# Decoder layer: output product in blocks of 512 columns scaled on VectorE, later routing pieces, first expert weights loaded from the last row tile, a unit of four experts last with its down weights in halves

## The chip, the cores and the metric

One core of one Trainium2 chip. The metric is the device time of one launch in microseconds, median of several runs. TensorE multiplies, VectorE and ScalarE work elementwise, GpSimd too, SyncE (SP) issues most of the transfers; each engine takes its instructions in the order in which the program wrote them. The profile's granted clock of TensorE is given as a share of its full speed.

## What is computed

One layer for a single sequence of 512 tokens of width 1024, float32. Two token mixers (a gated linear recurrence, HGRN2, and a sparse attention, NSA) are merged by sigmoid gates and go through one output product; then comes a mixture of experts, 32 experts in 4 groups, each token in 2 experts of its best group. The tail of the reference, which is what the change touches:

```python
merged = jax.nn.sigmoid(mg_h) * (o_h @ w_br_hg[l]) + jax.nn.sigmoid(mg_n) * (o_n @ w_br_nsa[l])
y = (1 + g1[:, None]) * (merged @ w_out[l])
x = _layer_norm(ALPHA * x + y) * ln1_g[l] + ln1_b[l]
h = _layer_norm(x) * (1 + sc2[:, None]) + sh2[:, None]
y = (1 + g2[:, None]) * _hier_moe(h, ...)      # softmax over groups, top 1; top 2 experts in it; SwiGLU
x = _layer_norm(ALPHA * x + y) * ln2_g[l] + ln2_b[l]
```

## The kernel before

Products of float32 precision are made of three TensorE passes: each operand is split into a rounded part and the rest (`wh`, `wl` for weights; ScalarE copies the rounded part, L275, VectorE subtracts it, L276), and `three_k` issues high by high, high by low and low by high. A `Block` holds the weights of one block of columns; it is loaded in pieces of 512 KB (`wst`), `np` pieces of `kp` row groups each. Weights with `early=True`, those of the output product `wo`, are first multiplied by the row 1 + g1 (`g1b`) on GpSimd, L274.

`run_jobs` runs a list of jobs in order and makes ready, beside each, the next blocks: their loads and splits are written between the matmuls of the jobs ahead. The last jobs are four merges of the first branch (`br_job(MGH, ...)`), the split of the attention's output (`onl`, L963), four merges of the second branch (`br_job(MGN, ...)`, which leave the merged rows split as `mh` and `ml`, L1091 and L1092) and the output product of row tile 0. `wo` is four blocks of 256 columns with two pieces each; two of these pieces are made ready in each of the four `MGN` merges.

Then a loop over the four row tiles of 128 tokens: `out_piece` makes the product of a tile with each of the four blocks of 256 columns (24 matmuls each), adds it to the residual `z` and takes statistics, for every 512 columns in the tiles 0 to 2, for every 256 in the last. After each tile but the last, its `ln` is spawned: LayerNorm 1, statistics of the second norm, eight transposes of `z` (`pzT`), logits (`plg`), choice of group and experts, rank of each token in its expert. `ln` is a generator; after each `yield` it goes on only when the planner's clock `W.clk`, which counts the estimated matmul time in ns, is later by the number yielded: `LN_T` (1000) ahead of the transposes, `LN_P` (3500) ahead of the logits, `LN_Q` and `LN_R` behind. `W.poll()` is called between pieces of the product. The last tile's `ln` (`last`) runs alone once all is drained.

Expert weights lie in the same 36 buffers of 128x1024 float32 (`Q`) as all else; a load is issued by SP, in order, and waits there until its buffer is free. The first unit's first four steps (eight loads) stand ahead of the loop over row tiles, the next (`load_unit((0, 1), LOADS[-1], 8, ...)`, eight loads) behind it, the first of these waiting for a buffer that the row tile 2 frees (`acc` out of `z`, L1203). The last four steps of the unit come after the last tile's routing.

Thirteen units follow, `[-2, -1] + ORDER`. The units -2 and -1 take the experts 0 to 3 in pairs, with 64 slots each; the others take the remaining experts by their number of tokens: 0 and 1 one expert with 128 slots, 2 to 6 two experts, 7 to 10 four experts with 32 slots each. All 32 experts are read, 12 loads of 512 KB each (`w1`, `w3`, `w2`, four steps each). `up` makes the SwiGLU product, `down` the second product, `combine` adds it to the rows (`acc`); for every second unit the rows of the next two units are gathered (`one_hots`, `gather`). The last unit is 6, two experts; its `w2` comes in quarters of 256 columns, rows of 1 KB, and the product, its scaling by weight and gate (`weighted_halves`) and the addition go quarter by quarter. Ahead of the last quarter's additions stands a loop for tokens beyond a unit's slots, which here runs no time (`overflow`). LayerNorm 2 closes the rows in eight pieces of 128x512, spread over VectorE, ScalarE and GpSimd by the list `CLOSE`; its gain and bias are read as two rows spread over 128 partitions by the DMA (`l2g`, `l2b`).

## Time and profile before

| | |
|---|---|
| time, median of 3 runs | 1269.35 us (1267.79 to 1269.76) |
| the profiled execution | 1270.81 us, span from the first to the last instruction 1268.6 us |
| TensorE busy | 1173.5 us (93%) |
| VectorE busy | 704.3 us (56%) |
| ScalarE busy | 427.2 us (34%) |
| GpSimd busy | 114.9 us (9%) |
| moved by DMA | 297.15 MB, of it expert weights 380 issues of 512 KB and some smaller |
| mean granted clock of TensorE | 0.982 |

A share over the whole span says little here, since the stages have different limits; the rows below are read by stretches of the span. Times in the rows are microseconds from the start of the span; where rows group instructions, the mean of one is in ns.

### The profile page before, as it was taken

What the parts mean: (1) busy time and instruction counts of PE and PEld (TensorE: products, weight loads), DVE (VectorE), ACT (ScalarE), POOL (GpSimd) and SP (SyncE); (2) the same over time, 40 slices, a digit from 0 to 9 for tenths busy, and PEclk for the clock granted to TensorE, in tenths of its full rate; (3) what the DMA queues carried; (4) which work ended last, traced back from release to release, by engine and by line L of the source; (5) the groups of instructions that cost most, each with busy time, mean ns of one, the idle gap of its engine ahead of it and who ended that gap; (6) DMA issues with size and microseconds to landing.
All of it is one profiled execution on the core that took longest, in us unless ns stands there. A gap on an engine that the chain in (4) does not pass through costs nothing. (4 is left out here: it accounts for less than half of the span.)

```text
span 1268.6 us, 18573 instructions
## 1 busy us (share of the span) xinstructions
PE 1173.5 (93%) x6647; PEld 813.2 (64%) x6647; DVE 704.3 (56%) x1645; ACT 427.2 (34%) x899; POOL 114.9 (9%) x176
## 2 busy tenths in 40 slices
...
GB/s 323 298 145 148 113 59 117 99 93 129 106 112 118 72 163 104 100 117 185 119 84 166 34 293 378 409 409 409 409 409 408 409 409 403 409 409 404 408 322 68
DMA packets 140926, 297.15 MB, mean 234 GB/s; under 512 B 11163, under 2 KB 83043, under 8 KB 140832
## 3 DMA queue, kind: packets, MB, share of 16 engines
...
q10 hardware_dynamic: 768, 2.37, 0.6%
...
q14 instruction: 41, 0.34, 0.1%
...
## 5 line engine op out<-in xcount | busy, mean ns | idle before, releaser
L183 PE MATMUL p<-ew,xe 128*32 128x512 f32 (+1 forms) x960 | 202.6, 597 | 14.0 <-DMA ew<-in_exp_w_dram 13.6
L276 DVE TENSOR_TENSOR wl<-wst,wh 128x1024 fp32r<-128x1024 f32 (+1 forms) x93 | 124.3, 1365 | 74.9 <-ACT wh L275 74.0
L183 PEld LDWEIGHTS p<-ew,xe 128*32 128x32 f32 (+1 forms) x960 | 54.1, 122 | 156.1 <-issue 80.4
L1514 DVE TENSOR_TENSOR s<-s,p 128x512 f32<-128x512 f32 x13 | 8.9, 688 | 189.3 <-PE p L183 173.6
L183 PE MATMUL py<-ew,aT 128*32 128x512 f32 (+2 forms) x496 | 98.8, 570 | 8.7 <-DMA ew<-in_exp_w_dram 5.9
L275 ACT ACTIVATE wh<-wst 128x1024 fp32r<-128x1024 f32 (+1 forms) x94 | 93.3, 1030 | 28.2 <-POOL wst L274 16.6
L183 PEld LDWEIGHTS py<-ew,aT 128*32 128x32 f32 (+1 forms) x496 | 27.1, 122 | 73.4 <-issue 33.4
L1522 ACT ACTIVATE aT<-pat 128x512 f32<-128x512 f32 x13 | 7.8, 597 | 186.5 <-PE pat L187 186.5
L1563 DVE TENSOR_TENSOR acc<-acc,pcb 128x512 f32<-128x512 f32 x96 | 58.3, 681 | 8.8 <-PE pcb L181 8.8
L1537 ACT ACTIVATE yh<-y 128x512 fp32r<-128x512 f32 (+1 forms) x28 | 16.8, 601 | 136.8 <-DVE y L1535 136.7
L181 PE MATMUL pgx<-pm,xhh 128*128 128x256 f32 (+1 forms) x224 | 55.7, 294 | 0.0
L181 PE MATMUL pgx<-pm,xhl 128*128 128x256 f32 (+1 forms) x224 | 54.2, 287 | 0.0
L514 POOL DMA_DIRECT2D adaw<-in_ada_w_dram x64 | 34.6, 543 | 195.6 <-PE ptp L187 43.7
L1535 DVE SCALAR_TENSOR_TENSOR y<-py,cs,g2b 128x512 f32<-128x512 f32 (+1 forms) x28 | 19.9, 711 | 58.4 <-PE py L183 58.2
L181 PE MATMUL pmg<-hh,wh 128*128 128x512 f32 x128 | 50.4, 394 | 0.0
L181 PE MATMUL psg<-hh,wh 128*128 128x512 f32 x128 | 50.3, 393 | 0.0
L181 PE MATMUL psg<-hl,wh 128*128 128x512 f32 x128 | 49.9, 390 | 0.0
L181 PE MATMUL pmg<-hh,wl 128*128 128x512 f32 x128 | 49.9, 390 | 0.0
L181 PE MATMUL psg<-hh,wl 128*128 128x512 f32 x128 | 49.9, 390 | 0.0
L181 PE MATMUL pmg<-hl,wh 128*128 128x512 f32 x128 | 49.8, 389 | 0.0
L181 PEld LDWEIGHTS pgx<-pm,xhh 128*128 128x128 f32 x224 | 43.6, 197 | 4.0 <-issue 2.3
L181 PE MATMUL pcb<-yh,pT 128*128 128x512 f32 (+1 forms) x112 | 43.7, 395 | 2.2 <-DVEq L1584 2.2
...
## 6 DMA issues: line engine op xcount, KB each, us to landing
ew<-in_exp_w_dram SPq DMA_DIRECT2D x380, 512.0 KB, 10.1
wst<-in_w_in_dram SPq DMA_DIRECT2D x66, 512.0 KB, 4.6
...
adaw<-in_ada_w_dram SPq DMA_DIRECT2D x16, 512.0 KB, 9.2
wst<-in_w_br_hg_dram SPq DMA_DIRECT2D x8, 512.0 KB, 6.6
wst<-in_w_br_nsa_dram SPq DMA_DIRECT2D x8, 512.0 KB, 4.4
wst<-in_w_out_dram SPq DMA_DIRECT2D x8, 512.0 KB, 4.5
...
```

The lines of the kernel that those rows point to most:

```text
L181: PE.matmul(o, l, r, start=start, stop=stop)
L183: PE.matmul(o, l, r, start=start, stop=stop, tile_position=pos)
L275: A.activation(wh, self.w[j], AF.Copy)
L276: (sub or V).tensor_sub(wl, self.w[j], wh.bitcast(F32))
L514: P_.dma_start(w, ada[:, k, 2048 + j * 512:2560 + j * 512])
L1514: V.tensor_mul(s1, s1, p3)
L1522: A.activation(aT, at_.rearrange("p (f s) -> p f s", f=4), AF.Copy)
L1535: V.scalar_tensor_tensor(y, py, cs_, g2b[c0 // 512][:, c0 % 512:c0 % 512 + n], op0=OP.mult, op1=OP.mult)
L1537: A.activation(yh, y, AF.Copy)
L1563: V.tensor_add(acc[i][:, s_], acc[i][:, s_], pc_)
```

## The change

The output product's weights become two blocks of 512 columns, with four pieces of two row groups each, and the multiplication by 1 + g1 moves from GpSimd to VectorE. The tiles 0 to 2 make two products of 512 columns, the last tile one of 512 and two of 256. `LN_T` goes from 1000 to 5000, `LN_P` from 3500 to 1500, and `proj_tok` with 512 columns yields after every second row group. The second batch of the first unit's loads is issued inside the last row tile, after its first 512 columns. In `ORDER` the unit 10, of four experts, comes last, and its `w2` is read in halves of 512 columns, two row groups to a load, rows of 2 KB. The last unit's rows are gathered inside the unit before it, between that unit's own two up products. Gain and bias of LayerNorm 2 are read as two rows of 4 KB, split, and spread over the partitions by TensorE. The end goes in two halves of 512 columns; the closing subtracts the mean and multiplies by the gain for whole rows on VectorE, then the tiles 0 and 1 are closed by a product with a diagonal matrix on TensorE, on top of the bias, and a copy by ScalarE, the tiles 2 and 3 by VectorE. `CLOSE` and GpSimd's part in it are gone. In the diff, a line of "..." marks what is left out.

```diff
@@ -65,15 +65,14 @@
...
-LN_T, LN_P, LN_Q, LN_L, LN_R = 1000, 3500, 800, 0, 3500
+LN_T, LN_P, LN_Q, LN_L, LN_R = 5000, 1500, 800, 0, 3500
...
-ORDER = [7, 0, 8, 1, 9, 2, 3, 10, 4, 5, 6]
+ORDER = [7, 0, 8, 1, 9, 2, 3, 4, 5, 6, 10]
...
-CLOSE = [(0, "VV"), (2, "AVP"), (3, "AVP"), (1, "VV"), (4, "AVP"), (6, "AVP"), (5, "VV"), (7, "VV")]
...
@@ -251,7 +250,7 @@
...
-            self.kp = {128: 8, 256: 4, 280: 2}[n]
+            self.kp = {128: 8, 256: 4, 280: 2, 512: 2}[n]
...
@@ -271,7 +270,7 @@
...
             if self.early:
-                P_.tensor_mul(self.w[j], self.w[j], g1b[:, None, self.c0:self.c0 + n].to_broadcast([128, kp, n]))
+                V.tensor_mul(self.w[j], self.w[j], g1b[:, None, self.c0:self.c0 + n].to_broadcast([128, kp, n]))
...
@@ -298,12 +297,12 @@
...
-    def proj_tok(b, ps, i, sh=None, sl=None, n=None):
+    def proj_tok(b, ps, i, sh=None, sl=None, n=None, c=0):
...
         for k in range(KT):
...
-                    lambda k: b.H(k, 0, n), lambda k: b.L(k, 0, n), k)
-            if k % 4 == 3:
+                    lambda k: b.H(k, c, n), lambda k: b.L(k, c, n), k)
+            if k % 4 == 3 or n == 512 and k % 2:
...
@@ -1100,7 +1099,7 @@
...
-    wo = [Block(vwo, c * 256, early=True) for c in range(4)]
+    wo = [Block(vwo, c * 512, 512, early=True) for c in range(2)]
...
@@ -1112,22 +1111,18 @@
...
-    def out_piece(b, i, q, width):
-        z, o = zs[i], q * 256 % width
-        if o == 0:
-            out_ps[i] = PS("pyo")[:, 0:width]
-        py = out_ps[i]
-        yield from proj_tok(b, py[:, o:o + 256], i, mh, ml)
-        if o + 256 == width:
-            s_ = slice(q * 256 + 256 - width, q * 256 + 256)
-            j = q * 256 // width
-            V.scalar_tensor_tensor(z[:, s_], z[:, s_], ALPHA, py, op0=OP.mult, op1=OP.add)
-            V.bn_stats(l1st[i][:, 6 * j:6 * j + 6], z[:, s_])
-    out_ps = {}
+    def out_piece(b, i, c, width):
+        z, n = zs[i], 256 if i + 1 == NT else 512
+        py = PS("pyo")[:, 0:width]
+        yield from proj_tok(b, py, i, mh, ml, width, c % 512)
+        s_ = slice(c, c + width)
+        V.scalar_tensor_tensor(z[:, s_], z[:, s_], ALPHA, py, op0=OP.mult, op1=OP.add)
+        for j in range(c // n, (c + width) // n):
+            V.bn_stats(l1st[i][:, 6 * j:6 * j + 6], z[:, j * n:(j + 1) * n])
...
-    jobs += [(wo[q], lambda b, q=q: out_piece(b, 0, q, 512), None) for q in range(4)]
+    jobs += [(wo[q], lambda b, q=q: out_piece(b, 0, q * 512, 512), None) for q in range(2)]
...
@@ -1287,7 +1282,7 @@
...
-    def load_unit(es, lo=0, hi=12, res=None, quarters=False):
+    def load_unit(es, lo=0, hi=12, res=None, halves=False):
...
         for t in range(lo, hi):
...
@@ -1302,10 +1297,11 @@
...
                 w = Q("ew")
-                if quarters and t >= 8:
-                    nc.sync.dma_start(w.rearrange("p (k n) -> p k n", k=4),
-                                      src.rearrange("p (k n) -> p k n", k=4)[:, :, j * 256:(j + 1) * 256])
+                if halves and t >= 8:
+                    kk, c0 = j % 2 * 2, j // 2 * 512
+                    nc.sync.dma_start(w.rearrange("p (k n) -> p k n", k=2),
+                                      src.rearrange("p (k n) -> p k n", k=4)[:, kk:kk + 2, c0:c0 + 512])
                 else:
                     nc.sync.dma_start(w, src[:, j * 1024:(j + 1) * 1024])
...
@@ -1319,14 +1315,16 @@
...
         if i:
-            for q in range(4):
-                for _ in out_piece(wo[q], i, q, width):
+            for c, w_ in ((0, 512), (512, 512)) if i + 1 < NT else ((0, 512), (512, 256), (768, 256)):
+                for _ in out_piece(wo[c // 512], i, c, w_):
...
+                if i + 1 == NT and c == 0:
+                    load_unit((0, 1), LOADS[-1], 8, w_first)
...
-    load_unit((0, 1), LOADS[-1], 8, w_first)
...
@@ -1601,7 +1599,7 @@
             combine(*down(act, {"exp_w2": [stream("exp_w2")]}, pw, lambda w, h: w(h)))
             for i in range(NT):
-                V.tensor_reduce(sums[:, i, 0:3], acc[i][:, 0:768].rearrange("p (q n) -> p q n", q=3), axis=AX.X, op=OP.add)
+                V.tensor_reduce(sums[:, i, 0:1], acc[i][:, 0:512], axis=AX.X, op=OP.add)
...
@@ -1623,8 +1621,26 @@
         def add_up():
             while todo:
                 combine(*todo.pop(0))
+        def next_hots():
+            nonlocal hots
+            for x in nxt:
+                rels[x] = rel_to(slots, 128.0 * x)
+            hots = one_hots([rels[x] for x in nxt])
         last = n + 1 == len(units)
-        act = up(xe, (n % 2) * 128, ws, mid=add_up if last else None)
+        nxt = units[n + 1:n + 3] if n % 2 == 1 else []
+        inside = len(nxt) == 1
+        xe_ = None
+        if inside:
+            next_hots()
+        def between():
+            nonlocal xe_
+            add_up()
+            if inside:
+                xe_ = gather(hots)
+        act = up(xe, (n % 2) * 128, ws, mid=between if last or inside else None)
         if last:
             break
         v_ = units[n + 1]
@@ -1636,119 +1652,122 @@
...
         else:
...
-        w_now, quarters = ws, n + 2 == len(units)
-        ws = load_unit(es, quarters=quarters)
+        w_now, halves = ws, n + 2 == len(units)
+        ws = load_unit(es, halves=halves)
...
-        nxt = units[n + 1:n + 3] if n % 2 == 1 else []
         def to_come():
-            nonlocal hots
...
-            if nxt:
-                for x in nxt:
-                    rels[x] = rel_to(slots, 128.0 * x)
-                hots = one_hots([rels[x] for x in nxt])
+            if nxt and not inside:
+                next_hots()
         todo.append(down(act, w_now, pw, mid=to_come))
         if nxt:
-            xe = gather(hots)
+            xe = xe_ if inside else gather(hots)
     w_now = ws
-    l2g = row_bc("l2g", a["ln2_g"])
-    l2b = row_bc("l2b", a["ln2_b"])
+    l2r = [Q(n_)[0:1, :] for n_ in ("l2gr", "l2br")]
+    for t, name in zip(l2r, ("ln2_g", "ln2_b")):
+        P_.dma_start(t, a[name])
...
-    sums = cp.tile([128, NT, 4], F32, name="sums")
+    sums = cp.tile([128, NT, 2], F32, name="sums")
...
-    def squares(i, half):
-        A.activation(sq, acc[i][:, half * 512:(half + 1) * 512], AF.Square, bias=nsh[:, i:i + 1],
-                     accum_out=sqs[:, i, half:half + 1])
-    def quarter_up(q):
-        py = PS("py")[:, 0:256]
+    halves_ = [slice(0, 512), slice(512, 1024)]
+    def squares(i, h):
+        A.activation(sq, acc[i][:, halves_[h]], AF.Square, bias=nsh[:, i:i + 1], accum_out=sqs[:, i, h:h + 1])
+    def half_up(h):
+        py = PS("py")
...
-                mm(py[m * x:m * x + m, :], aT[:, k, m * x:m * x + m], w[q][:, k * 256:(k + 1) * 256], k == 0, k == 3,
-                   pos=(0, m * x) if m < 128 else None)
+                mm(py[m * x:m * x + m, :], aT[:, k, m * x:m * x + m], w[2 * h + k // 2][:, k % 2 * 512:k % 2 * 512 + 512],
+                   k == 0, k == 3, pos=(0, m * x) if m < 128 else None)
...
-    def quarter_add(q, y, i):
-        pc_ = PS("pcb")[:, 0:256]
+    def half_add(h, y, i):
+        pc_ = PS("pcb")
...
-        z = acc[i][:, q * 256:(q + 1) * 256]
+        z = acc[i][:, halves_[h]]
...
-                               accum_out=sums[:, i, q:q + 1])
...
-    def quarter_y(q, py):
-        return weighted_halves(py, cs_, q * 256, 256)
-    py = quarter_up(0)
-    y = quarter_y(0, py)
...
+                               accum_out=sums[:, i, h:h + 1])
+    py = half_up(0)
+    y = weighted_halves(py, cs_, 0, 512)
+    oner = Q("oner", F32R)[0:1, 0:128]
+    A.activation(oner, ones[0:1, :], AF.Copy)
+    l2h, l2l = ([Q(n_, F32R)[0:1, :] for n_ in ns] for ns in (("l2gh", "l2bh"), ("l2gl", "l2bl")))
+    for t, h_, l_ in zip(l2r, l2h, l2l):
+        A.activation(h_, t, AF.Copy)
+        V.tensor_sub(l_, t, h_.bitcast(F32))
+    for i in range(NT):
+        half_add(0, y, i)
+    V.tensor_scalar(nsh, sums[:, :, 0], -1.0 / 512, None, op0=OP.mult)
+    l2g, l2b = Q("l2g"), Q("l2b")
+    for t, h_, l_ in zip((l2g, l2b), l2h, l2l):
+        for s_ in halves_:
+            ps = PS("pl2")
+            for j, x in enumerate((h_, l_)):
+                mm(ps, oner, x[:, s_], j == 0, j == 1)
+            A.activation(t[:, s_], ps, AF.Copy)
+    for i in range(NT):
+        squares(i, 0)
+    py = half_up(1)
+    y = weighted_halves(py, cs_, 512, 512)
     overflow()
...
-    V.tensor_reduce(l3[:, :, 4:5], sums[:, :, 0:3], axis=AX.X, op=OP.add)
     for i in range(NT):
-        quarter_add(3, y, i)
-    V.tensor_add(l3[:, :, 0], sums[:, :, 3], l3[:, :, 4])
+        half_add(1, y, i)
+        squares(i, 1)
+    V.tensor_add(l3[:, :, 0], sums[:, :, 0], sums[:, :, 1])
...
     V.tensor_mul(l3[:, :, 2], l3[:, :, 2], l3[:, :, 2])
     V.scalar_tensor_tensor(l3[:, :, 5], sqs[:, :, 0], 1.0 / D, l3[:, :, 2], op0=OP.mult, op1=OP.subtract)
...
-    for i in (0, 1):
-        squares(i, 1)
-    norm_scales(slice(0, 2))
-    for i in (2, 3):
-        squares(i, 1)
-    for j, (piece, how) in enumerate(CLOSE):
-        if j == 1:
-            norm_scales(slice(2, 4))
-        close(piece // 2, piece % 2, how)
+    def less_mean(i):
+        V.scalar_tensor_tensor(acc[i], acc[i], l3[:, i, 0:1], l2g, op0=OP.subtract, op1=OP.mult)
+    less_mean(0)
+    V.scalar_tensor_tensor(l3[:, :, 1], sqs[:, :, 1], 1.0 / D, l3[:, :, 5], op0=OP.mult, op1=OP.add)
+    A.activation(l3[:, :, 2], l3[:, :, 1], AF.Ln, bias=eps[:, 0:1])
+    A.activation(l3[:, :, 2], l3[:, :, 2], AF.Exp, scale=-0.5)
+    dg = S("dg")[:, 0:256].rearrange("p (i t) -> p i t", i=2)
+    pcl = {(i, h): PS("pcl") for i in range(2) for h in range(2)}
+    for (i, h), ps in pcl.items():
+        for j, b_ in enumerate((l2h[1], l2l[1])):
+            mm(ps, oner[:, 0:128], b_[:, halves_[h]], j == 0, False)
+    for i in range(2):
+        A.activation(dg[:, i, :], ident, AF.Copy, scale=l3[:, i, 2:3])
+    for i in range(1, NT):
+        less_mean(i)
+    for (i, h), ps in pcl.items():
+        z = acc[i][:, halves_[h]]
+        mm(ps, dg[:, i, :], z, False, True)
+        A.activation(z, ps, AF.Copy)
+        nc.sync.dma_start(out[0, i * 128:(i + 1) * 128, halves_[h]], z)
+    for i in range(2, NT):
+        for s_ in halves_:
+            z = acc[i][:, s_]
+            V.scalar_tensor_tensor(z, z, l3[:, i, 2:3], l2b[:, s_], op0=OP.mult, op1=OP.add)
+            nc.sync.dma_start(out[0, i * 128:(i + 1) * 128, s_], z)
...
```

## Rows read from the trace of the kernel before

**Rows 1.** Busy time by stretch: stretch, length, engines' busy us (instructions), clock, DMA share, GB/s.

```profile
582.00:625.00 43.00, 43.00 (x192) 35.37 (x190) 20.19 (x33) 15.66 (x16) 0.00 (x0) 1.00 0.34 110
625.00:681.35 56.35, 46.91 (x192) 36.90 (x192) 51.41 (x39) 15.41 (x18) 24.73 (x8) 0.94 0.39 127
681.35:745.70 64.35, 55.91 (x466) 53.85 (x464) 42.66 (x112) 20.08 (x32) 4.77 (x2) 0.97 0.37 130
744.00:746.00 2.00, 2.00 (x20) 1.88 (x18) 1.83 (x9) 1.97 (x3) 0.27 (x1) 1.00 1.04 422
745.70:764.60 18.90, 14.86 (x106) 13.58 (x104) 15.24 (x45) 8.18 (x13) 4.46 (x5) 0.73 1.02 373
776.00:1216.00 440.00, 414.98 (x2056) 179.03 (x2054) 171.09 (x404) 59.64 (x119) 0.28 (x1) 1.00 1.03 408
1216.00:1224.00 8.00, 8.00 (x37) 4.19 (x34) 2.73 (x5) 0.60 (x1) 0.78 (x2) 1.00 1.02 366
1224.00:1235.00 11.00, 9.83 (x54) 4.00 (x55) 3.45 (x6) 1.18 (x3) 0.00 (x0) 1.00 0.79 256
```

**Rows 2.** Groups of instructions, 625 to 681.35: count, busy us, mean ns, idle before.

```profile
L276 DVE TENSOR_TENSOR wl<-wst,wh 128x1024 fp32r<-128x1024 f32 x14 | 31.6, 2313 | 0.5 <-ACT wh L275 0.3 <-DMA wst<-in_w_out_dram 0.3
L274 POOL TENSOR_TENSOR wst<-wst,g1b 128x1024 f32<-128x1024 f32 x8 | 24.7, 3115 | 64.2 <-DVE onl L963 50.2 <-issue 7.3 <-DMA wst<-in_w_out_dram 6.7
L275 ACT ACTIVATE wh<-wst 128x1024 fp32r<-128x1024 f32 x12 | 11.9, 1046 | 16.6 <-POOL wst L274 16.6
```

**Rows 3.** Timeline of VectorE: start, us, instruction, count, idle before.

```profile
584.13 2.36 DVE L276 TENSOR_TENSOR wl<-wst,wh 128x1024 fp32r<-128x1024 f32 x2 [8.52 <-ACT wh L275]
...
630.08 13.43 DVE L276 TENSOR_TENSOR wl<-wst,wh 128x1024 fp32r<-128x1024 f32 x4
...
645.53 0.69 DVE L1092 TENSOR_TENSOR ml<-sgm,mh 128x512 fp32r<-128x512 f32 x1 [0.70 <-ACT mh L1091]
```

**Rows 4.** Timeline of TensorE in the second merge, its longest wait.

```profile
668.94 0.79 PE L181 MATMUL pbr<-onh,wl 128*128 128x512 f32 x1 [4.27 <-DVE wl L276]
```

**Rows 5.** Timeline of TensorE in the output product, two matmuls in a row.

```profile
700.49 0.28 PE L181 MATMUL pyo<-wh,ml 128*128 128x256 f32 x1
700.61 0.28 PE L181 MATMUL pyo<-wh,mh 128*128 128x256 f32 x1
```

**Rows 6.** TensorE's waits, 681.35 to 745.7: us in all, times, longest.

```profile
PE pzT L187 <- issue: 5.0, 2, 2.5
PE plg L183 <- ACT zT L1218: 2.1, 2, 1.1
```

**Rows 7.** Groups of the whole span (page, part 5), ScalarE's copy of 512 columns.

```profile
L1537 ACT ACTIVATE yh<-y 128x512 fp32r<-128x512 f32 (+1 forms) x28 | 16.8, 601 | 136.8 <-DVE y L1535 136.7
```

**Rows 8.** Timeline of VectorE, row tile 2 and the last tile.

```profile
733.04 1.28 DVE L1203 SCALAR_TENSOR_TENSOR acc<-z,l1mv,l1g 128x1024 f32<-128x1024 f32 x1
...
750.10 0.26 DVE L231 BATCH_NORM_AGGREGATE l1mv<-l1st 128x2 f32<-128x24 f32 x1
```

**Rows 9.** Waits of SP's DMA queue: us in all, times, longest.

```profile
SPq L1310 <- DVE acc L1203: 44.1, 1, 44.1
```

**Rows 10.** Timeline of VectorE and TensorE at the end.

```profile
1205.48 0.75 DVE L1535 SCALAR_TENSOR_TENSOR y<-py,cs,g2b 128x512 f32<-128x512 f32 x1 [2.51 <-PE py L183]
...
1221.27 4.87 DVE L1563 TENSOR_TENSOR acc<-acc,pcb 128x512 f32<-128x512 f32 x8 [8.77 <-PE pcb L181]
...
1233.82 3.67 PE L183 MATMUL py<-ew,aT 128*64 128x256 f32 x32 [0.31 <-ACT aT L1522]
...
1235.82 0.49 DVE L1535 SCALAR_TENSOR_TENSOR y<-py,cs,g2b 128x256 f32<-128x256 f32 x1 [0.74 <-PE py L183]
...
1248.43 0.17 DVE L1734 TENSOR_REDUCE l<-sums 128x4 f32<-128x12 f32 x1 [2.07 <-PE pcb L181]
...
1264.63 0.75 DVE L1707 SCALAR_TENSOR_TENSOR acc<-acc,l,l2b 128x512 f32<-128x512 f32 x1
```

**Rows 11.** DMA issues (page, part 6): count, size, median us to landing.

```profile
wst<-in_w_out_dram SPq DMA_DIRECT2D x8, 512.0 KB, 4.5
```

30 lines of the change are left out of this document (removed).

## The prediction

> **What bounds the kernel now.** I read the stages first, as busy time by stretch [rows 1]. From 776 to 1216 us the DMA engines move 408 GB/s at a share of 1.03, while TensorE, though called busy 94%, loads weights for only 179 of 440 us: the expert weights set the pace, every one of them is read whatever the routing, and the change removes none. So the time is where the stream starts, plus its bytes, plus what is left to do once it has ended. Before it lies a TensorE stage: the last merge of the branches (625.0 to 681.35) and the output product (681.35 to 745.7), 46.9 of 56.4 and 55.9 of 64.4 us busy. The merge of the other branch, the same 192 matmuls, took 43.0 us. Then a serial piece, 745.7 to 764.6, routes the last row tile. All weights that room can be found for are issued by 764.6, and the stream goes on only as the first unit uses buffers up, from 764.6. Hence the stream's end moves with that point, and an earlier load alone is worth nothing. At the end the last weights are in by 1235.0, and 33.6 us follow.
>
> **A. Scaling of the output weights on VectorE: +6.5 us.** GpSimd leaves the merge stage: 8 multiplies of 3.1 us, and beside them VectorE's 14 subtractions of 2.31 us on the mean [rows 2], where one alone takes 1.18 [rows 3]. But VectorE is in order, and it now does multiply, wait for ScalarE's copy, subtract: 1.2 (I take the subtraction's time) + 1.05 + 1.2 = 3.45 us a piece, 27.6 for eight. Blocks of 512 have four pieces, so all eight stand in the first two merge blocks; before, two pieces stood in each of four. VectorE comes out of the four `onl` at 630.1 [rows 3]. To the fourth block's first `wl` lie: 2.35 (two `wl` of the second block), 27.6, four merges of 0.69 + 0.69 + 0.70 waiting + 0.69 = 2.77 us [rows 3], together 11.1, the third block's copy and two `wl` less what overlaps, 2.7, and the fourth's copy and `wl`, 1.6. That is 45.3: 675.4. TensorE now waits for the same `wl` [rows 4] until 668.9, and has about 12.4 us of work behind it to 681.35, a slower clock included; so the stage ends near 687.8. Bounds: below, the twin stage's 43.0 us, a gain of 13.4; above, all eight subtractions still at 2.31, 9 us more, +15.5. I take the order of the code, +6.5.
>
> The Trainium skill (GPSIMD Engine Reference, section 4.1, Engine selection) says to put elementwise work on VectorE, since GpSimd is about twice as slow on two inputs. The rows agree on the instruction (3.1 against 1.2 us) and by that rule alone A would be a gain; it is the first rival.
>
> **B. Output product in 512 columns, routing later: -11.1 us.** A matmul of 256 columns starts 0.12 us after another [rows 5]: 384 are 46.1 us. One of 512 takes 43.0/192 = 0.224 [rows 1]: 168 of them and the 48 of 256 that the last tile keeps are 43.4, 2.7 less. TensorE idles 64.35 - 55.91 = 8.4 us in this stage [rows 1], 5.0 and 2.1 of it ahead of transposes and logits of the routing [rows 6] that were queued before VectorE or ScalarE had their input. With 5000 for 1000 on the planner's clock the transposes of a tile come a whole 512-column piece later (24 x 0.224 = 5.4 us), more than the 2.5 us that either wait lasted; the logits come 12 matmuls (2.7 us) behind, more than two copies of 0.6 us [rows 7]. I take all 8.4. Bounds: -2.7 (the waits only move) to -13.
>
> **C. The last tile's routing: +2.2 us.** Now the last row statistics start 4.4 us after TensorE's end [rows 8]. With the later delays the logits of the third tile come three quarters through the last piece, and their VectorE chain (L1228 to L1258, about 20 small instructions; 3.7 us, an estimate at 0.17 to 0.2 each, as the small one in [rows 10]) is queued ahead of the last residual add; the ranking of the third tile (1.7 to 3.3 us, an estimate for its nine by the same row) comes after it, and both ahead of the last statistics: 6.6 us. Bounds 0 and +4.
>
> So the first unit starts 6.5 - 11.1 + 2.2 = 2.4 us earlier. The second batch of eight loads is now held 44 us by buffers [rows 9]. In the change it is issued in the last row tile, about 10 us ahead of TensorE's end, as now (733.04 + 1.28 [rows 8], against 745.7): nothing won, but it must move along, since 20 loads and 1 MB of small ones (28 us at 408) have to fit before the first unit starts, and 30 us are there (734.4 to 764.6). Cover gone: each missing us is one us.
>
> **D. The stream itself: -7.5 us.** After 776 it carries 440 x 408 + 8 x 366 + 11 x 256 = 185.3 MB [rows 1]. Two broadcast rows of 0.5 MB each become two of 4 KB: 184.2 MB, at 408 GB/s 451.5 us, where it took 459.0. The slow end goes (256 GB/s at a share of 0.79 with rows of 1 KB): the last unit of four needs 61 us for its weights (48 of 512 KB) and some 29 of TensorE (144 matmuls at 415/2056 us), so loads no longer wait for TensorE, and its halves have rows of 2 KB, which moved 422 GB/s in the eight half-loads [rows 1]. Bounds: 0.4 more (no cost of the smaller rows) and 6 less (halves at 256/0.79 = 324 GB/s).
>
> **E. After the last weight: -12.3 us.** Now 33.6 us. In the change the first half's product, its adds and squares run while the last eight loads (10.3 us) arrive: 1.4 + 2.15 + 2.4 (two row splits) + 2.45 = 8.4 us on VectorE's side, hidden; if that cover is gone it costs what exceeds 10.3. After the landing: receipt 1.0 (an estimate, between 0 and the 3.2 us that hold a whole output after the last closing step, 1265.4 to the span's end [rows 10]), last matmuls 1.4 (between 0.5 and the 2.0 us that a whole quarter took from 1233.82 to 1235.82), y: 0.75 [rows 10] + 0.70 + 0.69 [rows 3] = 2.15, empty loop 2.1 (VectorE's idle time ahead of 1248.43), four adds at 4.87/8 = 0.61 [rows 10], five small ones 0.9, four subtractions of 1.28 [rows 8] at a step of 1.25 and one small 5.2, four closing halves at 0.7 (0.75 less what overlaps) 2.8, output 3.2: 21.2. ScalarE's squares end beside the small ones, and tiles 0 and 1 close on TensorE and ScalarE beside VectorE's subtractions (diagonal product and copy, four of each, ready some 1 us earlier than VectorE's last). GpSimd takes no part in it any more. The new matmuls that spread gain and bias (8) and their copies (4 of 0.6 us) lie ahead of the squares, in the same window. Bounds 18 and 27.
>
> **Sum.** 6.5 - 11.1 + 2.2 - 7.5 - 12.3 = -22.2 us on a span of 1268.6; the profiled run took 1270.81, 2.2 more, and the median of the runs lies 1.5 below it, at 1269.35. 1269.35 - 22.2 = 1247.
>
> **Rivals.**
> (1) The scaling is hidden: VectorE's chain keeps ahead of TensorE and A is a gain of about 11, 1230 us. For: GpSimd's contention goes, and ScalarE waited 16 us on it. Against: the order of the chain above. 12%.
> (2) The row tiles stay at their pace, since VectorE, not the order, sets it: 42.7 us busy in the product's 64.4 says no, but its chain per tile is long. B is -2.7: 1255.5. 14%.
> (3) TensorE's clock drops at the end. The granted clock was 0.73 in 745.7 to 764.6 after a pause, but 1.00 over 776 to 1216, through units that also waited for each load [rows 1]. At the lower level the last matmuls, the adds' and the diagonal products cost about 4 us more: 1251. 10%. The Trainium skill (TensorE: Matmul & The Clock Gate, section HAM oscillation) warns of just this, waits for DMA that throttle the engine each time; the long stretch at 1.00 here is against it.
> (4) Slower: room. All 36 buffers are in use when both blocks' eight pieces (three buffers each) stand beside two merge blocks and the split inputs. If VectorE's next multiply waits for a load that is itself waiting for a buffer, each such piece costs a landing of 4.5 us [rows 11]; from five on the gain is gone, with all eight 36 us: 1283. Against: buffers of the first branch come free at 625, before. 6%.
> That nothing measurable comes of it (the gains at the end eaten by A at its upper bound and a tail at 27): 3%.
>
> **Chances.** Forecast 53%, (1) 12, (2) 14, (3) 10, (4) 6, no change 3, faster still 2. 1234 to 1260 holds the forecast with its bounds, (2), (3) and a part of (1), about 8 in 10. Faster by over 0.2% (2.5 us, about what a measurement of this kernel can tell from no change) 0.91, within 0.03, slower 0.06.
>
> **What would show it.** A: in the merge stage a wait of TensorE for `wl` of 8 to 12 us ahead of the fourth block, and the stage at 60 to 65 us. B: the product from its first to its last matmul in about 53 us with no wait ahead of transposes. C: last statistics 6 to 7 us after the last product. D: 405 GB/s or more to within 2 us of the last landing. E: some 21 us from there to the end. Wrong if the loads in front leave a gap of the DMA engines behind the first unit's start, or if TensorE works on the last unit's up projections after its weights are in.

## The result, and the profile after

The changed kernel takes 1262.95 us (median of 5 runs, 1261.33 to 1264.07) where the kernel before took 1269.76 in the same comparison: a ratio of 0.9946, interval 0.9931 to 0.9961. It is 6.8 us faster; 22 were predicted, and the time lies above the range. The profiled execution took 1262.44 us, span 1260.7, so the spans differ by 7.9 us, and on them the terms can be compared:

| term | predicted | measured | from |
|---|---|---|---|
| A, end of the merge stage | +6.5 (687.8) | +6.4 (687.75) | first `pyo` |
| B, output product | -11.1 | -10.0 (54.35 for 64.35) | first to last `pyo` |
| C, last tile's routing | +2.2 | +2.3 (21.2 for 18.9) | last `pyo` to the first unit's first matmul |
| first unit's start | -2.4 | -1.3 (763.3 for 764.6) | |
| D, the stream | -7.5 | -5.7 | first unit to where the rate of the bytes ends, 1228.0 for 1235.0 |
| E, after the last weight | -12.3 (21.2) | -0.9 (32.7 for 33.6) | from there to the end of the span |

Four of five terms hold to within 2 us. The fifth, the largest, is off by 11.4 of the 14.3 us by which the sum missed on the spans.

The profile after, busy time by stretch (columns as in [rows 1]): merge, product, last tile, stream, the end of the rate, and what comes behind it.

```profile
624.20:687.75 63.55, 48.84 (x193) 38.07 (x193) 45.06 (x48) 16.68 (x19) 0.00 (x0) 0.89 0.45 147
687.75:742.10 54.35, 51.71 (x300) 43.02 (x299) 38.54 (x99) 16.77 (x29) 4.80 (x2) 1.00 0.37 126
742.10:763.30 21.20, 15.62 (x103) 14.20 (x101) 16.65 (x56) 10.61 (x15) 4.44 (x5) 0.68 0.91 328
776.00:1216.00 440.00, 417.23 (x2100) 184.84 (x2096) 175.48 (x413) 61.73 (x123) 1.01 (x2) 1.00 1.03 408
1216.00:1224.00 8.00, 6.25 (x29) 1.17 (x26) 0.46 (x1) 0.00 (x0) 0.00 (x0) 1.00 1.05 387
1226.00:1227.00 1.00, 0.77 (x3) 0.42 (x4) 0.58 (x1) 1.00 (x3) 0.00 (x0) 1.00 0.76 281
1227.00:1228.00 1.00, 1.00 (x6) 0.82 (x5) 0.96 (x1) 0.96 (x2) 0.00 (x0) 1.00 0.23 86
1228.00:1233.00 5.00, 5.00 (x33) 2.14 (x31) 3.99 (x11) 2.97 (x7) 0.00 (x0) 1.00 0.07 25
```

The merge stage got longer, 63.6 us, the product shorter and with hardly an idle moment (51.7 of 54.4 us busy); the stream keeps its 408 GB/s, but the last unit's halves move 387, not the 408 or 422 of [rows 1]. Beyond 1228 the rate is down to 25 GB/s at a share of 0.07, about what one of the 16 DMA engines moves (a sixteenth of 408 is 25.5): weights are still coming in.

VectorE in the merge (start, us, instruction, count, idle before), and TensorE at the same time:

```profile
654.09 1.22 DVE L273 TENSOR_TENSOR wst<-wst,g1b 128x1024 f32<-128x1024 f32 x1
656.50 1.22 DVE L275 TENSOR_TENSOR wl<-wst,wh 128x1024 fp32r<-128x1024 f32 x1 [1.19 <-ACT wh L274]
...
674.03 2.36 DVE L275 TENSOR_TENSOR wl<-wst,wh 128x1024 fp32r<-128x1024 f32 x2 [0.26 <-ACT wh L274]
```

```profile
674.05 0.80 PE L180 MATMUL pbr<-onh,wh 128*128 128x512 f32 x1 [9.12 <-ACT wh L274]
```

Multiply, 1.19 us of waiting for ScalarE's copy, subtract: this is a piece of the weights of the output product, 3.6 us, eight times. The fourth block's `wl` comes at 674.0 (675.4 was worked out), and TensorE waits 9.1 us, where [rows 4] had 4.3.

TensorE's waits inside the product (us in all, times, longest); [rows 6] had 5.0 and 2.1 us:

```profile
PE plg L182 <- ACT zT L1213: 2.6, 2, 1.5
```

The last unit's `w2`, sixteen loads, with the times of their issues and how long they take to land (us):

```profile
L1303 SPq DMA_DIRECT2D ew<-in_exp_w_dram x16: 372/412/909, 1202.0 to 1222.6; - x16
DMA to landing us min/median/max: 10.3/10.9/11.4
```

So the last load, issued at 1222.6, lands at about 1233.0, and not at 1228. In the trace's record of landings each load has sixteen; of the last load fifteen are in by 1228.8, the sixteenth at 1233.00.

The end, on four engines. TensorE first (`PEld` are its weight loads), then VectorE, ScalarE and SyncE:

```profile
1222.50 1.90 PE L182 MATMUL py<-ew,aT 128*32 128x512 f32 x10 [0.98 <-DMA ew<-in_exp_w_dram]
...
1230.49 4.46 PE L182 MATMUL py<-ew,aT 128*32 128x512 f32 x32
1233.05 0.17 PEld L182 LDWEIGHTS py<-ew,aT 128*32 128x32 f32 x8 [0.69 <-SPq L1582]
1240.07 0.79 PE L180 MATMUL pcb<-yh,pT 128*128 128x512 f32 x1 [5.12 <-issue]
...
1248.01 6.07 PE L180 MATMUL pcl<-acc,dg 128*128 128x512 f32 x8 [0.45 <-ACT dg L1758]
```

```profile
1234.99 0.75 DVE L1533 SCALAR_TENSOR_TENSOR y<-py,cs,g2b 128x512 f32<-128x512 f32 x1 [2.97 <-PE py L182]
...
1241.33 0.69 DVE L1707 CUSTOM_DVE_ANT_0 acc<-acc,pcb 128x512 f32<-128x512 f32 x1 [4.19 <-PE pcb L180]
...
1250.45 2.73 DVE L1769 SCALAR_TENSOR_TENSOR acc<-acc,l,l2b 128x512 f32<-128x512 f32 x4
```

```profile
1254.12 0.60 ACT L1764 ACTIVATE acc<-pcl 128x512 f32<-128x512 f32 x1 [0.26 <-PE pcl L180]
```

```profile
1250.75 4.33 SPq L1765 DMA_DIRECT2D out_dram<-acc  x4
1255.12 2.05 SPq L1770 DMA_DIRECT2D out_dram<-acc  x4
```

The first half's last weights were there at 1222.5, 10.5 us ahead of the second half's. The second half's product starts at 1230.5 and takes 4.5 us, and inside it TensorE waits for the last load: the weight load at 1233.05 waits for the semaphore of that load (the row names a queue of SyncE instead) and goes on 0.05 us after the landing. `y` follows at 1235.0. Then VectorE stands 4.19 us where [rows 10] had 2.07, and TensorE 5.12. TensorE comes back at 1240.07 with matmuls of 0.63 to 0.79 us, the lower of its two levels (1.2 GHz; granted clock 0.50 from 1240 to 1252), the diagonal products take 6.1 us, the last copy is done at 1254.7, and SyncE issues VectorE's four outputs only after it. Busy time while the outputs are written:

```profile
1250.00:1254.00 4.00, 4.00 (x7) 1.42 (x5) 3.18 (x5) 1.79 (x3) 0.00 (x0) 0.65 0.34 130
1256.00:1258.00 2.00, 0.00 (x0) 0.00 (x0) 0.00 (x0) 0.00 (x0) 0.00 (x0) 0.56 1.04 387
```

From 1250 to 1254, when half of the rows are ready, 130 GB/s are written; the bulk goes at 387 GB/s after 1256. The last thing to see is TensorE's branch at the empty loop (count, ns least, median and most, first and last start):

```profile
L1582 PEldq COMPARE_BRANCH  x3: 101/193/3281, 1233.2 to 1239.8; - x3
```

One of the three took 3.28 us. In the kernel before the longest took 0.31.

### The profile page after: what moved, and what is told of

It is laid out like the page before. It is cut to its first block, busy times and chain, and to the rows that moved or that the text cites. A ratio compares the mean times of both kernels' runs of the same rounds, so it can differ in the third digit from the quotient of the medians.

```text
span 1260.7 us, 18162 instructions
## 1 busy us (share of the span) xinstructions
PE 1174.7 (93%) x6455; PEld 805.9 (64%) x6455; DVE 691.6 (55%) x1626; ACT 431.3 (34%) x904; POOL 82.8 (7%) x164
## 5 line engine op out<-in xcount | busy, mean ns | idle before, releaser
L182 PE MATMUL p<-ew,xe 128*32 128x512 f32 (+1 forms) x960 | 195.4, 597 | 11.4 <-DMA ew<-in_exp_w_dram 11.0
L275 DVE TENSOR_TENSOR wl<-wst,wh 128x1024 fp32r<-128x1024 f32 (+1 forms) x93 | 109.5, 1200 | 84.5 <-ACT wh L274 83.8
L182 PE MATMUL py<-ew,aT 128*32 128x512 f32 (+1 forms) x464 | 96.4, 598 | 8.7 <-DMA ew<-in_exp_w_dram 5.8
L1535 ACT ACTIVATE yh<-y 128x512 fp32r<-128x512 f32 x26 | 16.4, 630 | 132.3 <-DVE y L1533 130.8
L1533 DVE SCALAR_TENSOR_TENSOR y<-py,cs,g2b 128x512 f32<-128x512 f32 x26 | 19.4, 748 | 62.2 <-PE py L182 62.0
L180 PE MATMUL pcb<-yh,pT 128*128 128x512 f32 x104 | 43.6, 420 | 6.6 <-issue 5.1
```

The costliest lines, as they stand in the source:

```text
L180: PE.matmul(o, l, r, start=start, stop=stop)
L182: PE.matmul(o, l, r, start=start, stop=stop, tile_position=pos)
L275: (sub or V).tensor_sub(wl, self.w[j], wh.bitcast(F32))
L1533: V.scalar_tensor_tensor(y, py, cs_, g2b[c0 // 512][:, c0 % 512:c0 % 512 + n], op0=OP.mult, op1=OP.mult)
L1535: A.activation(yh, y, AF.Copy)
```

## The experiments

Times are medians, each beside the kernel before on the same chip (1269.8 to 1272.3 us); ratios have their interval. "To unit" is the start of the first unit's first matmul in the profile, "rest" from there to the end of the span. The rest turned out very steady, 496.9 to 497.7 us in all kernels that leave the end as it is in effect, so it shows changes of the end to some tenths of a microsecond, while the part in front varied by 3 us between kernels that are alike there (762.5 to 765.4).

| kernel | time | ratio to before | to unit | rest |
|---|---|---|---|---|
| changed | 1262.95 | 0.9946 (0.9931 to 0.9961) | 763.3 | 497.4 |
| t_noloop | 1258.34 | 0.9896 (0.9876 to 0.9917) | 764.9 | 491.7 |
| t_spread | 1263.33 | 0.9938 (0.9917 to 0.9959) | 762.9 | 497.7 |
| t_outs | 1260.79 | 0.9921 (0.9898 to 0.9944) | 762.5 | 495.1 |
| h_mul | 1253.24 | 0.9853 (0.9830 to 0.9877) | 755.1 | 497.4 |
| h_gps | 1260.70 | 0.9926 (0.9909 to 0.9942) | 759.2 | 497.1 |
| h_delays | 1267.98 | 0.9988 (0.9973 to 1.0002) | 767.1 | 496.9 |
| h_load | 1263.60 | 0.9948 (0.9932 to 0.9965) | 763.6 | 497.2 |
| q_rows | 1263.92 | 0.9941 (0.9922 to 0.9960) | 764.9 | 500.5 |
| t_pad | 1260.53 | 0.9904 (0.9887 to 0.9920) | 764.9 | 494.2 |
| t_mid | 1262.98 | 0.9927 (0.9911 to 0.9944) | 763.9 | 497.5 |
| o_order | 1274.18 | 1.0025 (1.0012 to 1.0037) | 764.5 | 507.1 |
| best | 1250.83 | 0.9837 (0.9821 to 0.9853) | 752.8 | 495.3 |
| old_end | 1266.84 | 0.9970 (0.9960 to 0.9981) | 765.0 | 500.8 |
| t_warm | 1261.02 | 0.9922 (0.9906 to 0.9939) | 765.4 | 494.5 |
| best2 | 1248.55 | 0.9830 (0.9813 to 0.9846) | 753.6 | 492.4 |
| t_pad128 | 1263.32, one run | | 764.2 | 497.3 |
| t_pad32 | 1259.34, one run | | 763.4 | 494.1 |

All are edits of the changed kernel. In the expectations the end is counted from 1227.0, where the rate falls (33.7 us); the table of terms above counts from 1228.0, as the prediction did for the kernel before. Neither is the landing of the last weights. By the traces' landings that lies 469.1 to 469.7 us behind the first unit's start in the changed kernel and in every run that keeps its order and its halves, 473.8 in old_end and 473.1 in the kernel before.

### The end: the loop that runs no pass

**t_noloop** leaves the loop out.

```diff
-    overflow()
```

> The changed kernel (1262.95 us) with the loop for tokens beyond a unit's slots left out; it runs no pass here, so the work is the same. Theory: after the second half's `yl` (end 1237.13) TensorE stood until 1240.07 behind the loop's branch, one of which took 3.28 us, and fell to the lower clock in that pause. Without the loop the additions begin at once (VectorE idle 4.2 us becomes about 0.6), their step goes from 0.85 back to 0.61 us, the diagonal products from 6.1 to about 3.5 us: 1255 to 1257 us. Rival: the loop costs the 2.1 us of the prediction and the clock falls anyway, since TensorE has little to do there: 1261 us, with the diagonal products still at 6 us.

The rest is 5.7 us shorter. VectorE's first addition, and TensorE's diagonal products:

```profile
1238.85 0.69 DVE L1707 CUSTOM_DVE_ANT_0 acc<-acc,pcb 128x512 f32<-128x512 f32 x1 [0.59 <-PE pcb L180]
```

```profile
1244.79 5.21 PE L180 MATMUL pcl<-acc,dg 128*128 128x512 f32 x8 [2.52 <-ACT dg L1757]
```

The additions follow 0.59 us after `yl` at a step of 0.61. The diagonal products still take 5.2 us, since TensorE waited 2.5 us for the scales; the clock was back up for the last of them. So the empty loop, which runs no pass here, cost 5.7 us in all, some 3.6 of them as a pause (4.19 less 0.59) and the rest, by the shorter steps of additions and diagonal products, through the clock: the first theory, a little under its size, and the rival's 2.1 is out.

**t_pad**, **t_pad128**, **t_pad32** put small matmuls, whose result nobody reads, ahead of the first half's product, where TensorE waits for weights.

```diff
+    pad = PS("pad")
+    for _ in range(64):                  # 128 and 32 in the others
+        mm(pad[:, 0:32], onesb, strict[:, 0:32], True, True)
     py = half_up(0)
```

> The changed kernel with 64 small matmuls more on TensorE (32 columns, result unused), ahead of the first half's product, where TensorE waits for weights anyway. Theory: the 3.3 us of TensorE's branch out of the empty loop, which the kernel before (0.31 us) and the kernel with quarters (64 matmuls more, 0.31 us) don't have, hang on where in its instructions the loop lies, not on what is computed; with 64 more the branch takes 0.3 us, the first addition comes 2.1 us behind the second `yl` instead of 4.2, the clock's fall costs less: 1259 us. Rival: the branch hangs on TensorE's idle time or on the wait for the other engines; it stays at 3.3 us: 1263 us.

TensorE's branch and VectorE's first addition behind the loop, with 64:

```profile
L1582 PEldq COMPARE_BRANCH  x3: 97/187/310, 1234.5 to 1238.8; - x3
```

```profile
1240.57 0.69 DVE L1707 CUSTOM_DVE_ANT_0 acc<-acc,pcb 128x512 f32<-128x512 f32 x1 [2.11 <-PE pcb L180]
```

More work, and the end comes 3.2 us sooner: the branch takes 0.31 us again. Why it did so was open.

> As the kernel with 64 small matmuls ahead of the first half's product, but with 128 of them (3.5 us, still in the wait for weights). A matmul is two instructions on TensorE, so 64 move the loop by 128 instructions, 128 by 256. Theory (place in blocks of code): if TensorE's code comes in blocks, what counts is where a block ends; 256 instructions would move the loop by a whole block of the size that the Trainium skill gives (Runtime: NRT & Kernel Launch, section Instruction fetch mechanics: 16 KiB, 256 instructions), and the branch would take 3.3 us again. Rival (more code ahead or less idle time is what helps): with more of both the branch stays at 0.3 us.

> The same with 32 small matmuls (64 instructions). Theory (place in blocks): the branch takes one of the two values, 0.3 or 3.3 us, and nothing between. Rival (what helps is time or code in proportion): about 1.8 us.

The branch with 128, then with 32:

```profile
L1582 PEldq COMPARE_BRANCH  x3: 97/193/3301, 1234.1 to 1240.7; - x3
```

```profile
L1582 PEldq COMPARE_BRANCH  x3: 97/190/304, 1232.9 to 1237.1; - x3
```

It is 3.30 us with 128 and 0.30 with 32, nothing between. More code or more work ahead would not bring the 3.3 us back. It is the place of the loop in TensorE's instructions that decides, with a period that 256 instructions fit into. The traces show a transfer of code beside it: inside each of the eleven long branches lies a packet of 16 KB on an instruction queue of the DMA (in the changed kernel from 1236.1 to 1237.0, the branch from 1235.1 to 1238.4), and inside none of the seven short ones. The Trainium skill (Runtime: NRT & Kernel Launch, section Instruction fetch mechanics) says that code is refilled in blocks of 16 KiB, 256 instructions, and that a taken branch whose target is not in the window has to fetch it first; the four kernels and these packets agree with that. How the kernel before came to lie well, no run shows more of than its 0.31 us.

**t_warm** puts the 64 matmuls into the pause itself, behind `py = half_up(1)`.

```diff
+    pad = PS("pad")
+    for _ in range(64):
+        mm(pad[:, 0:32], onesb, strict[:, 0:32], True, True)
```

> The changed kernel with 64 small matmuls more on TensorE (32 columns, result unused), this time behind the second half's product, in the pause of the empty loop. Theory: they shift the loop as the other 64 did, so the branch takes 0.3 us, and they shorten TensorE's pause from 5.1 us to about 2, so that the clock stays up: the additions at a step of 0.61 us, the diagonal products' first at the full clock; 1258 us, about 2 less than with the 64 ahead of the first half. Rival: the clock falls in the wait for ScalarE's scales anyway, then as with the others: 1260.5 us; or TensorE reaches the loop so late that the additions wait for it: 1262 us.

TensorE at the additions, one of the slower ones:

```profile
1241.86 0.63 PE L180 MATMUL pcb<-yl,pT 128*128 128x512 f32 x1
```

The branch is short here too (0.40 us at most), and the clock lasts into the additions: the first matmuls start 0.23 us after one another and take 0.40, from 1241.86 on 0.43 and 0.63. The rest is 494.5 us, as with t_pad. The first rival holds: the clock falls in the end anyway, a little later.

### The end: queues of TensorE and SyncE

**t_spread** moves the splitting and spreading of gain and bias (L1713 to L1728) ahead of `py = half_up(0)`.

```diff
-    py = half_up(0)
-    y = weighted_halves(py, cs_, 0, 512)
...
     for t, h_, l_ in zip((l2g, l2b), l2h, l2l):
...
+    py = half_up(0)
+    y = weighted_halves(py, cs_, 0, 512)
     for i in range(NT):
         half_add(0, y, i)
```

> The changed kernel with the splitting and spreading of gain and bias moved ahead of the first half's product. Theory: the second half's product began at 1230.49 only because eight matmuls that spread the rows, and VectorE's two row splits of 1.2 us ahead of them, stood in the queues; it now begins behind the first half's additions at about 1228.4, the second `y` at 1232.9 instead of 1235.0, the time falls by 2.1 us to 1260.9. Rival: the last weights land only at about 1228 to 1230 and a wait on the DMA takes the place of the queue: a gain of 1 us or less, and the trace shows TensorE waiting for `ew` in the second half.

Busy time in the first half's product (the clock is the third figure from the end):

```profile
1218.00:1219.00 1.00, 1.00 (x4) 0.62 (x3) 0.22 (x1) 0.76 (x2) 0.00 (x0) 0.56 1.06 391
1223.00:1224.00 1.00, 1.00 (x8) 0.20 (x4) 0.00 (x0) 0.00 (x0) 0.00 (x0) 0.50 1.04 383
```

No gain. TensorE stands still up to 1217 for VectorE's splits, its clock falls to 0.50, the first half's product takes 6.1 us, the second half's begins at 1231.5 instead of 1230.5, and it comes to the last load's weights at 1232.9, 0.9 us after they landed. What the rival said of the weights holds all the same, and by more than it said: in the changed kernel the last ones landed at 1233.0, so the 2.1 us of the theory were not there to be won.

**t_mid** puts the eight matmuls between the two halves of the first half's product.

```diff
+            if k == 1 and mid:
+                mid()
-    py = half_up(0)
+    py = half_up(0, spread)
```

> The changed kernel with the spreading of gain and bias in the middle of the first half's product: half of its matmuls, the eight spreading ones, then the other half. Theory: spread ahead of the product, TensorE paused for VectorE's row splits and fell to the lower clock, which ate the gain; in the middle the pauses are those for the weights, the clock stays, and the second half's `y` comes 2.0 us earlier than in the changed kernel, 8.5 us behind the first instead of 10.55: 1261 us. Rival: the clock falls here too or the second half waits for its weights: no gain, 1263 us.

Busy time by stretch around the last weights of that half:

```profile
1222.00:1223.00 1.00, 0.18 (x4) 0.18 (x8) 0.00 (x0) 0.00 (x0) 0.00 (x0) 0.91 1.06 391
1223.00:1224.00 1.00, 1.00 (x8) 0.20 (x4) 0.00 (x0) 0.00 (x0) 0.00 (x0) 0.50 1.04 381
```

The pause is the same 0.98 us for the last weights as in the changed kernel, yet the clock falls, and the rest is 497.5. The second `y` is 9.3 us behind the first, but the first comes 1.7 us later. The second half's product begins at 1231.1 here, and it takes up the last load's weights at 1233.37, 0.05 us after they landed (469.4 us behind the first unit, as elsewhere). The rival's second reason holds: the second half waits for its weights, whatever stands ahead of it in TensorE's queue.

**t_outs** writes the closing in the order in which the rows are ready.

```diff
-    for (i, h), ps in pcl.items():
+    for i, h in ((0, 0), (2, 0), (2, 1), (0, 1), (3, 0), (3, 1), (1, 0), (1, 1)):
         z = acc[i][:, halves_[h]]
-        mm(ps, dg[:, i, :], z, False, True)
-        A.activation(z, ps, AF.Copy)
+        if i < 2:
+            mm(pcl[i, h], dg[:, i, :], z, False, True)
+            A.activation(z, pcl[i, h], AF.Copy)
+        else:
+            V.scalar_tensor_tensor(z, z, l3[:, i, 2:3], l2b[:, halves_[h]], op0=OP.mult, op1=OP.add)
         nc.sync.dma_start(out[0, i * 128:(i + 1) * 128, halves_[h]], z)
-    for i in range(2, NT):
...
```

> The changed kernel with the last eight outputs written in the order in which their rows are ready, VectorE's between ScalarE's, instead of tiles 0 and 1 first. Theory: the outputs of tiles 2 and 3 (rows ready from 1251.1 to 1253.2) waited on SyncE's queue behind tile 1 (ready at 1254.7), and the end lay 6.0 us behind the last closing step where it was 3.2 before; in order of readiness the end is 3.2 us behind 1254.7: 1260.2 us, 2.8 less. Rival: the queue is not the limit, the last outputs take what they take: no change.

Busy time by stretch, the same 4 us as above:

```profile
1250.00:1254.00 4.00, 3.07 (x5) 0.86 (x3) 2.06 (x4) 1.79 (x3) 0.00 (x0) 0.76 0.90 335
```

The same stretch of 4 us now moves 335 GB/s instead of 130 (from the first output's issue on 298 instead of 135), and the rest is 2.3 us shorter: the first theory, 0.5 short. The end is still 3.9 us behind the last copy (1253.7 to 1257.6): eight outputs of 256 KB ready within 4 us are 2.1 MB, 5.4 us at 387 GB/s.

**old_end** puts the whole end of the kernel before behind the new order: quarters, `CLOSE`, rows spread by the DMA. Its core:

```diff
+CLOSE = [(0, "VV"), (2, "AVP"), (3, "AVP"), (1, "VV"), (4, "AVP"), (6, "AVP"), (5, "VV"), (7, "VV")]
...
+                    nc.sync.dma_start(w.rearrange("p (k n) -> p k n", k=4),
+                                      src.rearrange("p (k n) -> p k n", k=4)[:, :, j * 256:(j + 1) * 256])
...
+    l2g = row_bc("l2g", a["ln2_g"])
+    l2b = row_bc("l2b", a["ln2_b"])
...
-    def half_up(h):
+    def quarter_up(q):
```

> The changed kernel with the whole end of the kernel before: quarters of `w2` and of the product, gain and bias spread by the DMA, closing by the old list on VectorE, ScalarE and GpSimd; unit 10 stays last. Theory: the new end, 33.7 us behind the last landing against 33.6 before, is worth nothing in itself; what is lost is only the 4 us of the stream with rows of 1 KB and the 1 MB of broadcast rows (2.5 us): 1266 to 1269 us. Rival: the new end is worth the 12 us that were predicted for it, the branch and the clock took them only in part, and the old end suffers from four experts in a quarter: 1275 us.

Busy time by stretch at the end of the bytes:

```profile
1234.00:1236.00 2.00, 2.00 (x22) 1.29 (x14) 0.48 (x1) 0.42 (x1) 0.00 (x0) 1.00 0.52 171
```

The time is the first theory's: 1266.84. The rate ends at about 1235, 470 us behind the first unit against 464.7, and 30.8 us follow, against 32.7. But the new end is not the longer one in itself, as that would have it: old_end has the short branch (0.32 us), the changed kernel the long one. Beside t_pad, which has the new end and a short branch, the rest of old_end is 6.6 us longer. By the last landing 4.4 of them lie in the stream (473.8 us behind the first unit against 469.4) and 2.2 behind it (27.0 us against 24.8). So both the stream and the end itself gain, and in the changed kernel the branch ate what the end gave.

### The stream's end

**q_rows** reads the last unit's `w2` in quarters and keeps halves for the product.

```diff
-                    kk, c0 = j % 2 * 2, j // 2 * 512
-                    nc.sync.dma_start(w.rearrange("p (k n) -> p k n", k=2),
-                                      src.rearrange("p (k n) -> p k n", k=4)[:, kk:kk + 2, c0:c0 + 512])
+                    nc.sync.dma_start(w.rearrange("p (k n) -> p k n", k=4),
+                                      src.rearrange("p (k n) -> p k n", k=4)[:, :, j * 256:(j + 1) * 256])
```

> The changed kernel with the last unit's `w2` read in quarters of 256 columns again (rows of 1 KB), two quarters to a half; order, unit and the rest as changed. Theory: the rows of 1 KB made the slow end of the kernel before; 16 loads of 0.52 MB at 324 GB/s instead of 387 take 26 us instead of 21.7: 4 us later, 1267 us. Rival: the end was slow because TensorE released buffers late in a unit of two experts; then the rows change nothing: 1263 us.

Busy time by stretch, then TensorE in the second half:

```profile
1226.00:1227.00 1.00, 1.00 (x10) 0.22 (x2) 0.00 (x0) 0.00 (x0) 0.00 (x0) 0.50 1.10 347
```

```profile
1235.71 6.20 PE L182 MATMUL py<-ew,aT 128*32 128x256 f32 x64
```

347 GB/s at a share of 1.10: the theory's cost shows in the rate, which ends about 6 us later in the profile, 4.4 more behind the first unit's start. In the time it is not shown. The last weights land only 1.5 us later (471.2 us behind the first unit against 469.7). The rest of 500.5 is that of the slowest of the four runs (1267.17), and what is long in it is TensorE: twice as many matmuls, whose second half starts at 1235.7 and takes 6.2 us at a clock of 0.50 to 1240. With so many more matmuls the loop lies elsewhere, and the branch takes 0.31 us, which gives back about 3 us (t_pad). The median is the rival's 1263, but not for the rival's reason.

**o_order** has the old `ORDER`, unit 6 of two experts last.

```diff
-ORDER = [7, 0, 8, 1, 9, 2, 3, 4, 5, 6, 10]
+ORDER = [7, 0, 8, 1, 9, 2, 3, 10, 4, 5, 6]
```

> The changed kernel with the order of units before, a unit of two experts last, its `w2` in halves. Theory: with two experts last TensorE releases buffers late (its matmuls take most of the unit's 31 us of weights) and loads wait for it; the last landing, 463.7 us behind the first unit's start now, comes 2 to 3 us later: 1265 us. Rival: the order gives nothing, rows of 2 KB were the whole gain of the stream's end: 1263 us, or less, since fewer weights then belong to the second half.

Busy time by stretch at the end of the bytes, then TensorE:

```profile
1226.00:1228.00 2.00, 1.43 (x8) 0.26 (x4) 0.45 (x1) 0.00 (x0) 0.00 (x0) 1.00 0.64 237
```

```profile
1220.34 7.09 PE L182 MATMUL p<-ew,xe 128*64 128x512 f32 x32
...
1229.72 3.65 PE L182 MATMUL py<-ew,aT 128*64 128x512 f32 x16 [0.25 <-ACT aT L1520]
```

Both theories are wrong. The bytes end no later (462 to 463 us behind the first unit's start), yet the kernel takes 11 us more than the changed one and is slower than the one before. TensorE is late: the last unit's second up product runs to 1227.4, when its weights have been there for long, and its own `w2` product starts at 1229.7. A matmul of a unit of two takes 0.22 us and one of four about 0.14, so 32 of them are 7.1 us against 4.5. With two experts last the end waits for TensorE, with four for the weights.

### In front: scaling, delays, loads

**h_mul** writes the multiplication one piece ahead.

```diff
-            if self.early:
-                V.tensor_mul(self.w[j], self.w[j], g1b[...])
+            while self.early and self.m < min(j + 2, self.np):
+                V.tensor_mul(self.w[self.m], self.w[self.m], g1b[...])
+                self.m += 1
```

> The changed kernel with VectorE's multiplication of a piece by 1 + g1 written one piece ahead, so that it multiplies the next piece while ScalarE copies this one. Theory: VectorE's chain of 45 us sets the merge stage (the fourth block's `wl` at 674.0, TensorE waiting 9.1 us for it), and 8 x 1.19 us of it is idle time behind ScalarE's copy; without that the wait is gone and the stage is 9 us shorter: 1254 us. Rival: the subtractions or the loads are the limit, or what is won in the stage is lost to buffers behind it (the DMA engines idle 3 us before the first unit already): 1259 us or more.

VectorE, then TensorE, in the merge:

```profile
654.09 1.22 DVE L272 TENSOR_TENSOR wst<-wst,g1b 128x1024 f32<-128x1024 f32 x1
655.23 1.22 DVE L275 TENSOR_TENSOR wl<-wst,wh 128x1024 fp32r<-128x1024 f32 x1
```

```profile
665.69 0.79 PE L180 MATMUL pbr<-onh,wh 128*128 128x512 f32 x1 [5.33 <-ACT wh L274]
```

VectorE multiplies the next piece while ScalarE copies this one, and the idle 1.19 us are gone. From the first `onh` matmul to the first `pyo` it is 54.0 us instead of 63.5: 9.5 = 8 x 1.19 less, and all of it arrives at the end: 1253.24 us.

**h_gps** gives the multiplication back to GpSimd, at its new place.

```diff
-                V.tensor_mul(self.w[j], self.w[j], g1b[:, None, self.c0:self.c0 + n].to_broadcast([128, kp, n]))
+                P_.tensor_mul(self.w[j], self.w[j], g1b[:, None, self.c0:self.c0 + n].to_broadcast([128, kp, n]))
```

> The changed kernel with the multiplication by 1 + g1 back on GpSimd, at the places where VectorE now does it. Theory: what costs is the place, eight pieces in the first two merge blocks, and VectorE's serial multiply, wait, subtract of 3.6 us a piece; GpSimd's multiplies of 3.1 us one after another give a chain of 25 to 28 us, a little shorter than VectorE's 29, with the subtractions slowed to 2.3 us: the fourth block's `wl` comes up to 4 us earlier, 1259 to 1262 us. Rival: the engine decides; on GpSimd each piece takes 3.1 + 1.05 + 2.3 us and the stage grows by another 5 us or more: 1268 us.

TensorE's waits in the merge and the product (us in all, times, longest):

```profile
PE pbr L180 <- ACT wh L274: 11.4, 2, 10.0
```

From the first `onh` matmul to the first `pyo` it is 60.0 us, 3.5 less than with VectorE (63.5), and the median is 2.3 us lower: the theory. TensorE still waits 10 us for the fourth block.

**h_delays** puts `LN_T, LN_P` back to 1000 and 3500.

```diff
-LN_T, LN_P, LN_Q, LN_L, LN_R = 5000, 1500, 800, 0, 3500
+LN_T, LN_P, LN_Q, LN_L, LN_R = 1000, 3500, 800, 0, 3500
```

> The changed kernel with the routing's delays back at 1000 and 3500. Theory: the later transposes are what took TensorE's 7 us of waits out of the row tiles; with the old delays they come back and the output product goes from 54.4 to about 61 us: 1270 us. Rival: blocks of 512 columns alone took them out, with fewer switches between pieces: 1263 us, no change.

TensorE's waits in the product:

```profile
PE pzT L186 <- DVE z L1120: 5.4, 2, 2.7
```

The waits ahead of the transposes are back (5.4 us; 0.3 in the changed kernel), the product takes 62 us for 54.4, the time is 5 us longer. The theory, 2 us under its size.

**h_load** issues the second batch behind the loop over row tiles again.

```diff
-                if i + 1 == NT and c == 0:
-                    load_unit((0, 1), LOADS[-1], 8, w_first)
...
+    load_unit((0, 1), LOADS[-1], 8, w_first)
```

> The changed kernel with the second batch of eight loads back behind the loop over row tiles. Theory: the stream goes on only when the first unit frees buffers, and the DMA engines idle about 3 us before that (761 to 767); loads issued some 5 to 8 us later fill that gap at first, and what is more than 3 us too late is lost: 1264 to 1268 us. Rival: the early load is worth its full earlier start, 8 us or more: 1271 us. Or it was worth nothing, another load bounds the start: 1263 us.

No change, 0.4 us under the theory's range, as in the last case that was named (another load bounds the start). The batch is issued 4 us later and fills the gap of the DMA engines ahead of the first unit: the share from 760 to 762 is 1.03 and 0.98 where the changed kernel had 0.67 and 0.25.

### Together

**best** is the edits of h_mul, t_outs and t_mid in one.

> Three changes together on the changed kernel: VectorE's multiplication one piece ahead (9.7 us less alone), the outputs in order of readiness (2 to 3 us less alone), the spreading in the middle of the first half's product (2 us by its theory). If they lie one behind the other on the path: 1253.2 - 2.5 - 2 = 1249 us; if the end gives only the larger of the last two: 1251 us.

**best2** is the edits of h_mul, t_outs and t_pad.

> VectorE's multiplication one piece ahead, outputs in order of readiness, and the 64 small matmuls ahead of the first half's product, on the changed kernel; the spreading stays where it was, since in the middle of the product it gained nothing. Theory: the three lie one behind the other, 9.7 + 2 to 3 + 2.5 to 4 us less than 1262.95: 1247 to 1249 us. Rival: the two at the end overlap, since both shorten the way to the last output of tile 1: 1250.8 us, as the combination without the 64 matmuls.

best has some 10 us in front and 2.1 at the end, as t_outs alone. best2 has 5.0 at the end: 2.3 + 3.2 less 0.5, so branch and outputs lie one behind the other. At 1248.55 us, 0.9830 of the kernel before, it is the fastest version, 14.4 us under the changed kernel.

## Why the prediction was wrong

**A was right, for its reason.** The order in VectorE's queue gave the stage's end, and h_mul took away exactly the wait that the step had named. That it came out to 0.1 us is luck: the `wl` came 1.4 us early, and the work behind it took 13.7 us for 12.4, with a granted clock of 0.50 from 674 to 678, after the wait. h_mul goes some way to the first rival (the scaling is hidden): its stage is 2.6 us shorter than in the kernel before (54.0 us against 56.6), where the rival had 11, and TensorE still waits 5.3 us. By the rule weighed there (the Trainium skill: GPSIMD Engine Reference, section 4.1, Engine selection) the move was a gain; here the trace agrees with it for one instruction and not for the stage, since GpSimd's 3.1 us went beside VectorE and VectorE's 1.2 went into its queue: 60.0 us against 63.5.

**B was right**, and h_delays shows that the waits left because of the delays: 5.4 us ahead of transposes come back with the old ones. Its 1.1 us of shortfall is 2.6 us of waiting for the logits that I had at nothing, less 1.5 us of work. **C was right** (+2.3): the aggregate of the last row statistics starts at 748.18, 6.1 us after the product's end at 742.10 (4.4 before, 6.6 in the sum), behind the logits' chain that the step had named; the other 0.6 us lie behind it.

**The stream: two steps were mis-sized.** The unit of four does what was said of it (o_order), but rows of 2 KB give 387 GB/s. The 422 was misread from [rows 1]: from 744 to 746 loads with rows of 4 KB were moving, since the half-loads were issued from 744.54 on and took 4.0 us or more to land. Where they do move, the kernel before has 343 GB/s at a full share:

```profile
748.00:750.00 2.00, 0.35 (x2) 0.35 (x3) 1.86 (x7) 0.00 (x0) 2.00 (x5) 0.50 1.07 343
```

And the DMA engines idle 3.1 us between 761 and 767 (a share of 0.48), where the kernel before has 0.9 between 764 and 770 (0.85): the loads in front were done before the first unit freed room. That is the gap which the prediction gave as a sign of being wrong. "Nothing won" by the earlier loads was right (h_load).

**E failed.** It was put as 21.2 us and took 32.7. The step was a chain of durations, and most of its durations were right: `y` 2.15, the small ones, the subtractions (4.87 for 5.2), the closing (2.73 for 2.8). What was wrong is four places where I took a wait or a pause over from the kernel before, or had none:
- From the end of the rate to the second `y`: 7.0 us, 2.4 in the sum (+4.6). The step took the end of the rate for the landing and added 1.0 us of receipt, at most 3.2. The last load landed at 1233.0, 5.0 us after the rate's end (+4.0), since one of the sixteen parts of each load comes late: in the changed kernel 4.2 us after the other fifteen for the last load. The matmuls behind it took 2.0 us for 1.4 (+0.6). "Hidden in 10.3 us" was right: the eighth of the sixteen loads landed 10.5 us before the last, VectorE was done with the first half at 1232.0, and it then stood idle for 2.97 us ahead of the second `y`. In the kernel before the last landing is at 1237.6, 2.6 us after 1235.0, but TensorE takes those weights only at 1241.6, so no wait told of it. Why one part is late, the runs don't show.
- The empty loop: 4.2 us for 2.1 (+2.1). The 2.07 of [rows 10] was taken as a property of the loop; it is one of the place of the code (t_pad).
- The clock: additions at a step of 0.85 us for 0.61 (+0.8), and the diagonal products, which were to be ready 1 us before VectorE's last row and came 1.5 us after it (+1.5). That is the third rival, at 10%, with 2.3 us for its 4. The prediction held against it that the clock was 1.00 over 776 to 1216; the fall came where TensorE had nothing to do for 5 us, and the longest pause of the stream there is 0.98 us.
- The outputs: 6.0 us for 3.2 (+2.8). The 3.2 was one output's time at the end of a closing that took 13 us. Eight outputs within 4 us are bound by their bytes, and half of them stood behind the last copy on SyncE's queue (t_outs, 2.3 us).

Smaller differences take off 0.4, and that is the 11.4 to 11.5 us. Of these, the loop with what hangs on the clock (3.2, t_pad) and the outputs (2.3, t_outs) were won back by runs, and 5.0 by both together (best2). The first place was not: t_spread and t_mid moved TensorE's matmuls, and the landing stayed.

Counted from the last landing, the changed kernel has 27.7 us to the end where the kernel before has 31.0. So the end took 3.3 us less even with the long branch in it, and the stream 3.4 less (469.7 for 473.1 us behind the first unit); the table's -0.9 and -5.7 split the same gain at the end of the rate.

The chances erred in one way: the rivals were set against single terms, and none said that the largest term, a new end that no row had shown, could be worth nothing as a whole.
